# RWKV-7 recurrence in chunks: small matrix products interleaved over the four quadrants of the array, and the inverse's lanes loaded by two plain transfers

## The chip, the cores and the metric

The kernel runs on one core of one Trainium2 chip. The metric is the device time of one execution in microseconds (us), the median over several executions. The profile comes from one more execution, recorded by the hardware profiler; its engines are called PE (TensorE matmul; PEld is its weight load), DVE (VectorE), ACT (ScalarE), POOL (GpSimd) and SP (SyncE, which here only issues transfers).

## The reference, cut to what matters

A trunk of two layers on a 1024 x 1024 fp32 input (1024 tokens). The even layer has a gated MLP over chunks and a dilated attention; the odd layer is RWKV-7 time mixing with 16 heads of 64 channels. The change touches the odd layer's recurrence only:

```python
def rwkv7_scan(r, w, k, v, kk, a):            # (S, B, H, N), state (B, H, N_v, N_k)
    def step(state, inp):
        r_t, w_t, k_t, v_t, kk_t, a_t = inp
        sa = jnp.einsum('bhvk,bhk->bhv', state, -kk_t)
        state = (state * w_t[:, :, None, :]
                 + sa[..., None] * (kk_t * a_t)[:, :, None, :]
                 + v_t[..., None] * k_t[:, :, None, :])
        y_t = jnp.einsum('bhvk,bhk->bhv', state, r_t)
        return state, y_t
    _, ys = lax.scan(step, state0, (r, w, k, v, kk, a))
    return ys
```

After it come a group norm of y, a bonus term, a SiLU gate, an output projection, a residual add and a final norm.

## The kernel before, in words

The program runs in stages: the even layer to about 508 us, the odd layer's projections to about 1003 us, the recurrence to about 1390 us, then the output projection and the end. The recurrence (class `Rwkv`) doesn't go token by token. It takes the 1024 tokens in 16 chunks of 64, and turns the dependences within a chunk into a triangular 64 x 64 inverse per head. Heads are laid out as 8 pairs `q`, and in a pair head `e` (0 or 1) has partitions 64e to 64e+63. So each product of one head is 64 x 64 and uses one quadrant of the 128 x 128 array: rows are chosen by the partitions of the operands, columns by the partitions of the output. A block of such products is 16 instructions (8 pairs, 2 heads). Blocks whose head `e` goes from rows e to columns e use the two diagonal quadrants; blocks from rows e to columns 1-e, the other two.

For one chunk `c` the blocks are, with the lines of the kernel before:

- `al` (`alphas`, L1051, evacuated to M at L1052): products of A and BK for the inverse, diagonal. `ak` (`keys`, L1040, to AK at L1041): products of BK and A, off the diagonal. Both go through the PSUM tag "pt" with two buffers.
- `sc` (`scores`, L1029, to MY at L1030): 8 products of 128 x 64 for half of the pairs.
- `sM` (`store_M`, L1059): four transfers from ACT's queue put the 32 x 32 blocks of M to DRAM (MA). `lM` (`load_M`, L1098, on SP's queue) reads them back as lanes, one per partition, into Nt; a lane's 1024 numbers are contiguous, and partitions 64 to 127 hold the same as 0 to 63.
- `ia`, `ie`, `ib`, `ic`: VectorE inverts the lanes (DN at L1120, tm and R to L1163, result xm); `ic` stores xm to XT (L1170, SP), `lX` loads it as X (L1178, four transfers on SP). `mx`, `ma`, `mb` (L1184, L1196, L1209) merge the 32 x 32 blocks to the 64 x 64 inverse.
- `V` (`Wkeys`, L1223, off the diagonal) and `W` (L1230, diagonal) sum into one PSUM tile, evacuated to Ws (L1232). `U` (L1241, diagonal) applies X to Ws and is evacuated to UV (L1244). `st` (`state`, L1265, then an add on VectorE, L1267) makes the next state S; `keep` decays it on GpSimd.
- `Y` (`Yout`): L1275 from MY and UV, then L1280 from the state, then the evacuation (L1281). `Yd` stores Y (L1285, ACT's queue).

One step of the loop takes two chunks, and prepares the chunks of two steps later: its M blocks are made while the inverse of the step between is under way. The order in which every engine gets its instructions is the order of the program, written out by hand in three strings of tokens (SCAN_START, SCAN_STEP for six steps, SCAN_END); a token is a function's short name with a number. The gate projection of the odd layer is cut into pieces (`g`, L943, six or nine 128 x 512 matmuls at a time), which stand between the tokens. One inverse is in flight at a time (Nt has one buffer, X one). The six steps' strings before:

```python
SCAN_STEP = (
    "U0 V1 al0 ib2 st0 al1 sM0 uv0 Y0 keep1 ib1 W1 sc0 ib1 U1 V2 ak0 uv1 ld6 st1 sc1 ib1 ic0 dec0 Y1 lM0 W2 keep2 ip0 "
    "lX0 ak1 gx1 sc2 Yd0 T0 msk0 g2 ia0 sc3 g2 mx0 ma0 ie0 g2 dec1 T1 mb0 msk1 g3 ib3 ld7 gl2")
```

Of the kernel before, what the change touches and what calls it, by code (L numbers as in the profile page):

```python
# [11 lines left out]
AF = mybir.ActivationFunctionType  # L12
# [12 lines left out]
NC = 16  # L25
CH = 64
# [201 lines left out]
def even_layer(g, a):  # L228
# [749 lines left out]
class Rwkv:  # L978
# [39 lines left out]
    def scores(self, c, qq):  # L1018

        g, nc, t = self.g, self.g.nc, self.T[c]  # L1020
        A, BK = t["A"], t["BK"]
        if qq == 0:
            t["MY"] = self.ring("MY", c, NY, [P, NHD, CH])
        pm = self.pm[:, :, qq]
        for i in range(4):
            q = 4 * qq + i
            for e in range(2):
                r = slice(64 * e, 64 * e + 64)
                nc.tensor.matmul(pm[:, e, i], BK[r, q].rearrange("p j t -> p (j t)"), A[r, q, 1], start=True, stop=True)  # L1029
        nc.scalar.activation(t["MY"].rearrange("p (e q) t -> p e q t", e=2)[:, :, 4 * qq:4 * qq + 4], pm, AF.Copy)  # L1030

    def keys(self, c):

        g, nc, t = self.g, self.g.nc, self.T[c]
        t["AK"] = AK = self.ring("AK", c // 2, 3, [P, 2, KT, CH])[:, c % 2]
        pk = g.bC([P, KT, CH], "pt")
        for q in range(KT):
            for e in range(2):
                r, o = slice(64 * e, 64 * e + 64), slice(64 - 64 * e, 128 - 64 * e)
                nc.tensor.matmul(pk[o, q], t["BK"][r, q, 1 - e], t["A"][r, q, 0], start=True, stop=True)  # L1040
        nc.scalar.activation(AK, pk, AF.Copy)  # L1041

    def alphas(self, c):

        g, nc, t = self.g, self.g.nc, self.T[c]
        M = self.ring("M", c // 2, 2, [P, 2, KT, CH])
        pa = g.bC([P, KT, CH], "pt")
        for q in range(KT):
            for e in range(2):
                r = slice(64 * e, 64 * e + 64)  # L1050
                nc.tensor.matmul(pa[r, q], t["A"][r, q, 0], t["BK"][r, q, e], start=True, stop=True)  # L1051
        nc.scalar.activation(M[:, c % 2], pa, AF.Copy)  # L1052
# [39 lines left out]
    def load_M(self, b2):  # L1092

        g, nc, pool = self.g, self.g.nc, self.pool
        Nf = pool.tile([P, 1056], F32, name="Nt", bufs=1)
        Nt = Nf[:, 0:1024].rearrange("p (t s) -> p t s", s=32)
        m = g.MA_d[b2]
        nc.sync.dma_start(Nf[:, 0:1024], bass.AP(tensor=m.tensor, offset=m.offset, ap=[[0, 2], [1024, 64], [1, 1024]]))  # L1098
# [116 lines left out]

    def Wkeys(self, c):

        g, nc, t = self.g, self.g.nc, self.T[c]
        self.pw = g.bA([P, KT, CH], "ch")
        for q in range(KT):  # L1220
            for e in range(2):
                o, r = slice(64 * e, 64 * e + 64), slice(64 - 64 * e, 128 - 64 * e)
                nc.tensor.matmul(self.pw[o, q], t["AK"][r, q], t["UV"][r, e, q], start=q == 0, stop=False)  # L1223

    def W(self, c):
        g, nc, t = self.g, self.g.nc, self.T[c]
        for q in range(KT):
            for e in range(2):
                o = slice(64 * e, 64 * e + 64)
                nc.tensor.matmul(self.pw[o, q], t["A"][o, q, 0], t["S"][o, q],  # L1230
                                 start=False, stop=q == KT - 1)
        nc.scalar.activation(self.Ws, self.pw, AF.Copy)  # L1232

    def U(self, c):
        g, nc, t = self.g, self.g.nc, self.T[c]
        X = self.ring("X", c // 2, 1, None)
        pu = g.bA([P, KT, CH], "ch")
        for q in range(KT):
            for e in range(2):
                o = slice(64 * e, 64 * e + 64)  # L1240
                nc.tensor.matmul(pu[o, q], X[o, c % 2, q], self.Ws[o, q], start=True, stop=True)  # L1241
        for e in range(2):
            o = slice(64 * e, 64 * e + 64)
            nc.scalar.activation(t["UV"][o, e], pu[o], AF.Copy)  # L1244
# [24 lines left out]
    def Yout(self, c):  # L1269

        g, nc, t = self.g, self.g.nc, self.T[c]
        py = g.bD([P, KT, CH], "py")
        for q in range(KT):
            for e in range(2):
                nc.tensor.matmul(py[64 * e:64 * e + 64, q], t["MY"][:, 8 * e + q], t["UV"][:, e, q],  # L1275
                                 start=q == 0, stop=False)
        for q in range(KT):
            for e in range(2):
                r = slice(64 * e, 64 * e + 64)
                nc.tensor.matmul(py[r, q], t["A"][r, q, 1], t["S"][r, q], start=False, stop=q == KT - 1)  # L1280
        nc.scalar.activation(self.Y[:, c % 2], py, AF.Copy)  # L1281

    def store_Y(self, b):
        for e in range(2):
            self.g.nc.scalar.dma_start(self.g.Y_d[b].rearrange("(c t) h d -> t c h d", c=2)[:, :, 8 * e:8 * e + 8],  # L1285
                                     self.Y[64 * e:64 * e + 64])

    def start(self, gate):
        g, nc = self.g, self.g.nc

        def zs(i):
            nc.gpsimd.memset(self.new_S(0), 0.0)

        self.pm = g.bB([P, 2, 2, 4, CH], "pm")
        ops = dict(L=gate.load, wx=gate.split, xl=gate.load_x, ld=self.load,
                   g=lambda i: [next(gate.rest, None) for _ in range(i)],
                   sc=lambda i: self.scores(i // 2, i % 2), al=self.alphas, sM=self.store_M, lM=self.load_M,
                   ip=self.inverse_p, ia=self.inverse_a, ie=self.inverse_d, ib=lambda i: [next(self.rows, None) for _ in range(i)],
                   ic=self.inverse_c, lX=self.load_X, mx=self.merge_x, ma=self.merge_a, mb=self.merge_b,
                   dec=self.decayed, T=self.transposed, msk=self.masks,  # L1300
                   ak=self.keys, uv=self.load_uv, V=self.Wkeys, W=self.W, keep=self.keep, zs=zs)
        for name, i in order(SCAN_START):
            ops[name](i)

    def ops(self, b, gate):
        c = 2 * b
        return dict(
            U=lambda i: self.U(c + i), st=lambda i: self.state(c + i), keep=lambda i: self.keep(c + i),
            W=lambda i: self.W(c + i), V=lambda i: self.Wkeys(c + i), sc=lambda i: self.scores(c + 4 + i // 2, i % 2),
            al=lambda i: self.alphas(c + 4 + i), sM=lambda i: self.store_M(b + 2 + i),  # L1310
            lM=lambda i: self.load_M(b + 2 + i), ip=lambda i: self.inverse_p(b + 2 + i),
            ia=lambda i: self.inverse_a(b + 2 + i),
# [2 lines left out]
            mx=lambda i: self.merge_x(b + 1 + i), ma=lambda i: self.merge_a(b + 1 + i),  # L1315
            mb=lambda i: self.merge_b(b + 1 + i), dec=lambda i: self.decayed(c + 4 + i),
            T=lambda i: self.transposed(c + 4 + i), Y=lambda i: self.Yout(c + i),
            msk=lambda i: self.masks(c + 4 + i), ak=lambda i: self.keys(c + 4 + i),
            uv=lambda i: self.load_uv(c + 2 + i), ld=lambda i: c + i < NC and self.load(c + i),
            g=lambda i: [next(gate.rest, None) for _ in range(i)],  # L1320
            gl=lambda i: b + KT + i < 2 * KT and gate.load(b + KT + i),
# [226 lines left out]
```

## Time and profile before

| | before |
|---|---|
| median of three runs | 1547.66 us (1547.51 to 1555.07) |
| the profiled execution | 1541.35 us |
| its span | 1539.6 us |
| mean granted clock of TensorE | 0.94 |
| busy share of the span | PE 88%, DVE 57%, ACT 41%, POOL 35% |

The recurrence is a quarter of the span. The profile gives a page, and for any stretch: a timeline by engine (start, duration, line, out<-in, and in brackets the idle time ahead with what ended it), the chain of work that ended last, a table of waits, and windows with the busy time of each engine, the clock that TensorE was granted, and the share of the 16 DMA engines that was busy. A matmul row counts records; neighbouring records of one line are put together as "x32".

### The profile page before, as it was taken

The page shows a single profiled execution, that of the slowest core. Times are in us where ns is not written, and L with a number is a line of the kernel's source. Part 1 is how long each engine was busy: PE and PEld are TensorE (multiplying, and loading weights), DVE is VectorE, ACT ScalarE, POOL GpSimd, SP SyncE. Part 2 cuts the span into 40 slices and gives each one's busy share as a digit, 9 for nine tenths or more (in the row PEclk, how much of TensorE's full clock was granted, in tenths as well). Part 3 has the DMA queues.
Part 4 walks back from the last instruction along what each step waited for, and adds up shares of the span by engine and source line. Part 5 has one row for each costly group of instructions (what it writes and reads, how often), then busy time and mean ns, then how long its engine had stood idle before and what let it go on. Part 6 is the DMA issues. An engine that isn't in the chain of part 4 may idle for free.

```text
span 1539.6 us, 29856 instructions
## 1 busy us (share of the span) xinstructions
PE 1349.7 (88%) x12261; PEld 1154.1 (75%) x12261; DVE 885.2 (57%) x1489; ACT 631.7 (41%) x1188; POOL 545.9 (35%) x353
## 2 busy tenths in 40 slices
PE   5899999799979999999978799988977777687887
PEld 5887879688878899888645478967866666677886
DVE  8742446834574357615988974315554544477884
ACT  4423436533543235626454542323433333254322
POOL 8650001120216212213433531227323333357851
PEclk9999999999999999999989899989988888889899
DMA  5385444521523443241865474265744445476412
GB/s 212 100 268 152 124 155 119 138 69 53 154 82 131 138 130 98 66 140 42 232 185 124 109 206 114 64 198 135 237 118 131 111 125 139 120 222 217 139 40 96
DMA packets 253032, 209.09 MB, mean 136 GB/s; under 512 B 79408, under 2 KB 215184, under 8 KB 252896
## 3 DMA queue, kind: packets, MB, share of 16 engines
q1 hardware_dynamic: 230096, 191.98, 42.2%
q10 hardware_dynamic: 22800, 15.21, 3.6%
q8 instruction: 96, 1.57, 0.4%
q14 instruction: 40, 0.33, 0.1%
HBM read 135.71 MB, written 71.43 MB: 135 GB/s over the span
## 4 chain that ended last, share of the span: by engine, by line
PE 57%; DVE 15%; DMA 10%; issue 5%; ACT 5%; POOL 3%; SPq 3%; ACTq 1%; DVEq 0%; POOLq 0%
PE pj L153 34%; PE pj L943 3%; DMA X<-XT 3%; SPq L1178 2%; PE pj L1460 1%; PE pt L572 1%; PE pj L711 1%; PE pm L1029 1%; DMA BK<-BK_d 1%; DMA Nt<-MA 1%; PE pt L1051 1%; PE sp L559 1%; PE ch L1241 1%; PE sp L562 1%; PE op L580 1%
## 5 line engine op out<-in xcount | busy, mean ns | idle before, releaser
L106 POOL TENSOR_TENSOR wl<-wraw,wh 128x1024 fp32r<-128x1024 f32 x38 | 95.5, 2514 | 176.0 <-ACT wh L105 159.3
L153 PE MATMUL pj<-hh,wh 128*128 128x512 f32 x320 | 127.3, 398 | 0.0
L153 PE MATMUL pj<-hh,wl 128*128 128x512 f32 x320 | 126.7, 396 | 0.0
L153 PE MATMUL pj<-hl,wh 128*128 128x512 f32 x320 | 126.6, 396 | 0.0
L106 DVE TENSOR_TENSOR wl<-wraw,wh 128x1024 fp32r<-128x1024 f32 x46 | 69.8, 1523 | 87.4 <-ACT wh L105 43.8
L105 ACT ACTIVATE wh<-wraw 128x1024 fp32r<-128x1024 f32 x84 | 88.0, 1055 | 60.6 <-DMA wraw<-in_w_in_even_dram 22.2
L153 PE MATMUL pj<-xl,wh 128*128 128x512 f32 x256 | 103.2, 404 | 2.6 <-DVE xl L740 2.6
L153 PE MATMUL pj<-xh,wh 128*128 128x512 f32 x256 | 103.1, 405 | 2.5 <-ACT ks L789 2.4
L153 PE MATMUL pj<-xh,wl 128*128 128x512 f32 x256 | 102.8, 402 | 0.0
L1460 PE MATMUL pj<-wh,yh 128*128 128x256 f32 x256 | 76.9, 300 | 5.4 <-DVE x L1464 3.2
L566 DVE CUSTOM_DVE_ANT_0 sc<-sp,tb 128x128 f32<-128x128 f32 (+3 forms) x64 | 48.2, 753 | 57.7 <-PE sp L562 48.9
L1460 PE MATMUL pj<-wh,yl 128*128 128x256 f32 x256 | 75.9, 296 | 5.6 <-POOL yl L106 5.6
L153 PE MATMUL pj<-wh,hh 128*128 128x256 f32 x256 | 74.8, 295 | 2.9 <-ACT hh L265 2.6
L153 PE MATMUL pj<-wh,hl 128*128 128x256 f32 x256 | 75.0, 294 | 1.2 <-DVE hl L266 1.2
L1460 PE MATMUL pj<-wl,yh 128*128 128x256 f32 x256 | 75.5, 295 | 0.0
L737 DVE SCALAR_TENSOR_TENSOR xm<-hT,pr,xm 128x512 f32<-128x512 f32 x56 | 50.0, 934 | 44.0 <-ACT xm L736 43.6
L153 PE MATMUL pj<-wl,hh 128*128 128x256 f32 x256 | 74.4, 291 | 0.0
L153 PE MATMUL pj<-wh,yl 128*128 128x256 f32 x256 | 72.5, 283 | 1.9 <-POOL yl L624 1.9
L153 PE MATMUL pj<-wh,xh 128*128 128x256 f32 x256 | 72.9, 285 | 0.1
L153 PE MATMUL pj<-wl,xh 128*128 128x256 f32 x256 | 72.9, 285 | 0.0
L153 PE MATMUL pj<-wh,xl 128*128 128x256 f32 x256 | 72.8, 284 | 0.0
L153 PE MATMUL pj<-wh,yh 128*128 128x256 f32 x256 | 72.1, 282 | 0.5 <-ACT yh L623 0.5
(320 smaller groups left out, 4034.3 us busy)
## 6 DMA issues: line engine op xcount, KB each, us to landing
wraw<-in_w_in_even_dram SPq DMA_DIRECT2D x28, 512.0 KB
tb<-tb SPq DMA_DIRECT2D x16, 512.0 KB
A_d<-AR SPq DMA_DIRECT2D x16, 512.0 KB
wraw<-in_rw_wg_dram SPq DMA_DIRECT2D x16, 512.0 KB
A<-A_d SPq DMA_DIRECT2D x16, 512.0 KB
BK<-BK_d SPq DMA_DIRECT2D x16, 512.0 KB
xt<-in_x_dram SPq DMA_DIRECT2D x8, 512.0 KB
dv<-vt SPq DMA_DIRECT2D x16, 256.0 KB
```

The lines of the kernel that those rows point to most:

```text
L105: nc.scalar.activation(hi, raw, AF.Copy)
L106: sub.tensor_tensor(lo, raw, hi.bitcast(F32), OP.subtract)
L153: nc.tensor.matmul(ps, a(k), b(k), start=(n == 0), stop=(n == 3 * KT - 1))
L559: nc.tensor.matmul(sp[:, c0:c1], qs[:, b * P:(b + 1) * P], kh[:, c0:c1], start=True, stop=False)
L562: nc.tensor.matmul(sp[:, c0:c1], qs[:, b * P:(b + 1) * P], kl[:, c0:c1], start=False, stop=True)
L566: nc.vector.tensor_tensor_reduce(sc[:, :n], sp[:, :n], tb[:, off:off + n], 1.0, BIG, OP.add, OP.min, mn)
L572: nc.tensor.transpose(pt[:, j - j0, :], sc[:, j * P:(j + 1) * P], g.ident)
L580: nc.tensor.matmul(op[:, s0:QW], vt[:, j, :], pth[j // 4][:, j % 4, s0:QW], start=(j == 0), stop=False)
L737: nc.vector.scalar_tensor_tensor(t, hT[kk, f][:, j, 0:512], g.pr[:, i, k:k + 1], t, op0=OP.mult, op1=OP.add)
L943: nc.tensor.matmul(ps, u[:, k], v[:, k % 2], start=(k == 0 and i == 0), stop=(k == KT - 1 and i == 2))
L1178: self.g.nc.sync.dma_start(X[32 * k:32 * k + 32, :, :, 32 * b:32 * b + 32].rearrange("p c q t -> p (c q) t"), xd[k].rearrange("c q a e t - ...
L1460: nc.tensor.matmul(ps[:, i, :], u[:, k], v[:, k % 4], start=(k == 0 and j == 0), stop=(k == KT - 1 and j == 2))
```

## The change

It does three things. The load of the lanes is written as two transfers of 64 partitions x 1024 numbers instead of one with a leading dimension of 2 and stride 0. Blocks on the diagonal quadrants and blocks on the other two are issued alternately, pair by pair: `al` with `ak` of the same chunk (both now evacuated there, so the token `ak` goes away), `U` of a chunk with `V` of the next, and `W` of a chunk with the state half of `Y` of the chunk before. For the last, the halves of the PSUM tile of Y and of its store are swapped. `sc` is written as 16 products of 64 x 64 over all quadrants instead of 8 of 128 x 64.

```diff
 SCAN_STEP = (
-    "U0 V1 al0 ib2 st0 al1 sM0 uv0 Y0 keep1 ib1 W1 sc0 ib1 U1 V2 ak0 uv1 ld6 st1 sc1 ib1 ic0 dec0 Y1 lM0 W2 keep2 ip0 "
-    "lX0 ak1 gx1 sc2 Yd0 T0 msk0 g2 ia0 sc3 g2 mx0 ma0 ie0 g2 dec1 T1 mb0 msk1 g3 ib3 ld7 gl2")
+    "U0 al0 ib2 st0 al1 sM0 uv0 Y0 keep1 ib1 W1 sc0 ib1 U1 uv1 ld6 st1 sc1 ib1 ic0 dec0 Y1 lM0 W2 keep2 ip0 lX0 "
+    "gx1 sc2 Yd0 T0 msk0 g2 ia0 sc3 g2 mx0 ma0 ie0 g2 dec1 T1 mb0 msk1 g3 ib3 ld7 gl2")
...
     def scores(self, c, qq):
...
-            for e in range(2):
-                r = slice(64 * e, 64 * e + 64)
-                nc.tensor.matmul(pm[:, e, i], BK[r, q].rearrange("p j t -> p (j t)"), A[r, q, 1], start=True, stop=True)
+            for j in range(2):
+                for e in range(2):
+                    r, o = slice(64 * e, 64 * e + 64), slice(64 * (e ^ j), 64 * (e ^ j) + 64)
+                    nc.tensor.matmul(pm[o, e, i], BK[r, q, e ^ j], A[r, q, 1], start=True, stop=True)
...
     def alphas(self, c):
-        pa = g.bC([P, KT, CH], "pt")
+        t["AK"] = AK = self.ring("AK", c // 2, 3, [P, 2, KT, CH])[:, c % 2]
+        pa, pk = g.bC([P, KT, CH], "pt"), g.bC([P, KT, CH], "pt")
         for q in range(KT):
             for e in range(2):
                 r = slice(64 * e, 64 * e + 64)
                 nc.tensor.matmul(pa[r, q], t["A"][r, q, 0], t["BK"][r, q, e], start=True, stop=True)
+            for e in range(2):
+                r, o = slice(64 * e, 64 * e + 64), slice(64 - 64 * e, 128 - 64 * e)
+                nc.tensor.matmul(pk[o, q], t["BK"][r, q, 1 - e], t["A"][r, q, 0], start=True, stop=True)
         nc.scalar.activation(M[:, c % 2], pa, AF.Copy)
+        nc.scalar.activation(AK, pk, AF.Copy)
...
     def load_M(self, b2):
-        nc.sync.dma_start(Nf[:, 0:1024], bass.AP(tensor=m.tensor, offset=m.offset, ap=[[0, 2], [1024, 64], [1, 1024]]))
+        for par in range(2):
+            nc.sync.dma_start(Nf[64 * par:64 * par + 64, 0:1024], m.rearrange("k c q t s -> (k c q) (t s)"))
...
     def Wkeys(self, c):
         for q in range(KT):
...
+            yield
     def W(self, c):
+        rest = self.Ystate(c - 1) if c else iter(())
         for q in range(KT):
...
+            next(rest, None)
         nc.scalar.activation(self.Ws, self.pw, AF.Copy)
+        next(rest, None)
     def U(self, c):
+        rest = self.Wkeys(c + 1) if c < NC - 1 else iter(())
         for q in range(KT):
...
+            next(rest, None)
...
     def Yout(self, c):
...
+    def Ystate(self, c):
+        py, Y = self.py, self.Y
+        for q in range(KT):
+            for e in range(2):
+                r, o = slice(64 * e, 64 * e + 64), slice(64 - 64 * e, 128 - 64 * e)
+                nc.tensor.matmul(py[o, q], t["A"][r, q, 1], t["S"][r, q], start=False, stop=q == KT - 1)
+            if q < KT - 1:
+                yield
+        yield
+        nc.scalar.activation(Y[:, c % 2], py, AF.Copy)
```

On TensorE, the beginning of a step before, from the first U to the second (ch, pt, py and pm are PSUM tiles; MATMUL rows give output <- operands):

```order
L1241 MATMUL ch<-Ws,X 64x64 x16
L1223 MATMUL ch<-UV,AK 64x64 x16
L1051 MATMUL pt<-BK,A 64x64 x16
L1265 MATMUL ch<-UV,BKT 64x64 x16
L1051 MATMUL pt<-BK,A 64x64 x16
L1275 MATMUL py<-UV,MY 64x64 x16
L1280 MATMUL py<-S,A 64x64 x16
L1230 MATMUL ch<-S,A 64x64 x16
L1029 MATMUL pm<-A,BK 128x64 x8
L1241 MATMUL ch<-Ws,X 64x64 x16
```

In the changed kernel every block of 16 that has a partner is cut into twos, which alternate with its partner's; this is where the second U with V ends, and the following W with the state half of Y begins:

```order
L1246 MATMUL ch<-Ws,X 64x64 x2
L1221 MATMUL ch<-UV,AK 64x64 x2
L1271 MATMUL ch<-UV,BKT 64x64 x16
L1030 MATMUL pm<-A,BK 64x64 x16
L1281 MATMUL py<-UV,MY 64x64 x16
L1231 MATMUL ch<-S,A 64x64 x2
L1290 MATMUL py<-S,A 64x64 x2
```

V is no longer a block of its own between U and the state's product (L1265 before, L1271 now), nor is `ak`, which stood there in the second half of the step. On SP's queue, at the end of an inverse in the middle of a step (store of XT, load of the next lanes, load of X, loads of the next chunks):

```order
 L1003 DMA BK<-BK_d 128x1024
-L1170 DMA XT_138<-xm 1024x1x32 x2
-L1098 DMA Nt<-MA_131 128x1x1024
-L1178 DMA X<-XT_138 32x16x32 x4
+L1167 DMA XT_138<-xm 1024x1x32 x2
+L1095 DMA Nt<-MA_131 64x1024 x2
+L1175 DMA X<-XT_138 32x16x32 x4
 L1001 DMA A<-A_d 128x1024
```

The places on the queue stay; only the load of the lanes has become two. On ACT, between the first and the second U's evacuation of a step, before:

```order
L1244 ACTIVATE UV<-ch 64x512 x2
L1052 ACTIVATE M<-pt 128x512 x2
L1059 DMA MA_132<-M 32x16x32 x4
L1281 ACTIVATE Y<-py 128x512
L1232 ACTIVATE Ws<-ch 128x512
L1030 ACTIVATE MY<-pm 128x2x256
```

and now:

```order
L1250 ACTIVATE UV<-ch 64x512 x2
L1047 ACTIVATE M<-pt 128x512
L1048 ACTIVATE AK<-pt 128x512
L1047 ACTIVATE M<-pt 128x512
L1048 ACTIVATE AK<-pt 128x512
L1055 DMA MA_132<-M 32x16x32 x4
L1234 ACTIVATE Ws<-ch 128x512
L1294 ACTIVATE Y<-py 128x512
L1031 ACTIVATE MY<-pm 128x2x256
```

Two evacuations of AK have come ahead of the stores of M, and the evacuation of Y has moved behind that of Ws.

More of the change, by code (lines that the diff above doesn't have):

```diff
@@ L1026, in scores @@
             q = 4 * qq + i
-            for e in range(2):
-                r = slice(64 * e, 64 * e + 64)
-                nc.tensor.matmul(pm[:, e, i], BK[r, q].rearrange("p j t -> p (j t)"), A[r, q, 1], start=True, stop=True)
+            for j in range(2):
+                for e in range(2):
+                    r, o = slice(64 * e, 64 * e + 64), slice(64 * (e ^ j), 64 * (e ^ j) + 64)
+                    nc.tensor.matmul(pm[o, e, i], BK[r, q, e ^ j], A[r, q, 1], start=True, stop=True)
         nc.scalar.activation(t["MY"].rearrange("p (e q) t -> p e q t", e=2)[:, :, 4 * qq:4 * qq + 4], pm, AF.Copy)
[L1032 to L1041, printed above, removed]
     def alphas(self, c):
@@ L1218, in Wkeys @@
         g, nc, t = self.g, self.g.nc, self.T[c]
-        self.pw = g.bA([P, KT, CH], "ch")
+        self.pw = pw = g.bA([P, KT, CH], "ch")
         for q in range(KT):
@@ L1222, in Wkeys @@
                 o, r = slice(64 * e, 64 * e + 64), slice(64 - 64 * e, 128 - 64 * e)
-                nc.tensor.matmul(self.pw[o, q], t["AK"][r, q], t["UV"][r, e, q], start=q == 0, stop=False)
+                nc.tensor.matmul(pw[o, q], t["AK"][r, q], t["UV"][r, e, q], start=q == 0, stop=False)
+            yield
     def W(self, c):
         g, nc, t = self.g, self.g.nc, self.T[c]
+        rest = self.Ystate(c - 1) if c else iter(())
         for q in range(KT):
@@ L1271, in Yout @@
         g, nc, t = self.g, self.g.nc, self.T[c]
-        py = g.bD([P, KT, CH], "py")
+        self.py = g.bD([P, KT, CH], "py")
         for q in range(KT):
             for e in range(2):
-                nc.tensor.matmul(py[64 * e:64 * e + 64, q], t["MY"][:, 8 * e + q], t["UV"][:, e, q],
+                nc.tensor.matmul(self.py[64 - 64 * e:128 - 64 * e, q], t["MY"][:, 8 * e + q], t["UV"][:, e, q],
                                  start=q == 0, stop=False)
+    def Ystate(self, c):
+        g, nc, t = self.g, self.g.nc, self.T[c]
+        py, Y = self.py, self.Y
         for q in range(KT):
             for e in range(2):
-                r = slice(64 * e, 64 * e + 64)
-                nc.tensor.matmul(py[r, q], t["A"][r, q, 1], t["S"][r, q], start=False, stop=q == KT - 1)
-        nc.scalar.activation(self.Y[:, c % 2], py, AF.Copy)
+                r, o = slice(64 * e, 64 * e + 64), slice(64 - 64 * e, 128 - 64 * e)
[4 more added lines that the diff above has]
+        nc.scalar.activation(Y[:, c % 2], py, AF.Copy)
     def store_Y(self, b):
@@ L1285, in store_Y @@
             self.g.nc.scalar.dma_start(self.g.Y_d[b].rearrange("(c t) h d -> t c h d", c=2)[:, :, 8 * e:8 * e + 8],
-                                     self.Y[64 * e:64 * e + 64])
+                                     self.Y[64 - 64 * e:128 - 64 * e])
     def start(self, gate):
@@ L1300, in start @@
                    dec=self.decayed, T=self.transposed, msk=self.masks,
-                   ak=self.keys, uv=self.load_uv, V=self.Wkeys, W=self.W, keep=self.keep, zs=zs)
+                   uv=self.load_uv, V=lambda i: list(self.Wkeys(i)), W=self.W, keep=self.keep, zs=zs)
         for name, i in order(SCAN_START):
@@ L1308, in ops @@
             U=lambda i: self.U(c + i), st=lambda i: self.state(c + i), keep=lambda i: self.keep(c + i),
-            W=lambda i: self.W(c + i), V=lambda i: self.Wkeys(c + i), sc=lambda i: self.scores(c + 4 + i // 2, i % 2),
+            W=lambda i: self.W(c + i), sc=lambda i: self.scores(c + 4 + i // 2, i % 2),
             al=lambda i: self.alphas(c + 4 + i), sM=lambda i: self.store_M(b + 2 + i),
@@ L1317, in ops @@
             T=lambda i: self.transposed(c + 4 + i), Y=lambda i: self.Yout(c + i),
-            msk=lambda i: self.masks(c + 4 + i), ak=lambda i: self.keys(c + 4 + i),
+            msk=lambda i: self.masks(c + 4 + i), R=lambda i: list(self.Ystate(c + i)),
             uv=lambda i: self.load_uv(c + 2 + i), ld=lambda i: c + i < NC and self.load(c + i),
```

18 rows, old and new, of tables (SCAN_END, SCAN_START) are left out of this document.

## The prediction

> **What bounds the kernel now.** I read the page first (TensorE busy 88% of the span), then the granted clock, the chain of waits, the table of waits and the queue timeline of the recurrence only, because the change touches nothing else. The chain of waits gives the recurrence's period. These are the first and the last of five consecutive starts of the merge's first product (L1196), with the pieces that follow one of them; columns are start, duration, what.
>
> ```profile
> 1124.69 1.91 PE pt L1196 x62
> ...
> 1134.23 0.90 PE ch L1241 x26
> ...
> 1136.83 1.08 PE ch L1265 x32
> ...
> 1146.02 0.93 PE pt L1040 x32
> ...
> 1148.03 1.04 PE pm L1029 x16
> ...
> 1153.96 1.02 PE pt L1076 x8
> 1154.99 1.38 PE pj L943 x6
> ...
> 1167.94 1.91 PE pt L1196 x62
> 1169.86 2.86 PE pj L943 x6
> 1172.71 1.58 PE pt L1076 x8
> ...
> 1177.74 0.90 PE ch L1241 x26
> ...
> 1296.44 1.91 PE pt L1196 x62
> ```
>
> A step (two chunks) takes (1296.44 − 1124.69)/4 = 42.94 us. I cut it in three: **b**, from the first U (1134.23) to the issue of the inverse's store XT; **c**, from that issue to the merge; **a**, from the merge to the next U (1177.74 − 1167.94 = 9.8). The queue of SP, with start and duration:
>
> ```profile
> 1150.72 1.27 SPq L1170 DMA_DIRECT2D XT<-xm  x2
> 1152.09 0.56 SPq L1098 DMA_DIRECT2D Nt<-MA  x1
> 1154.36 8.96 SPq L1178 DMA_DIRECT2D X<-XT  x4
> ```
>
> So b = 1150.72 − 1134.23 = 16.5 and c = 1167.94 − 1150.72 = 17.2. In c the four small X loads alone hold SP for 8.96 us, and the lanes' load Nt stands ahead of them. The table of waits of 1003 to 1390 us shows who waits (total, times, longest), and the windows show busy time of PE, PEld, DVE, ACT, POOL, then granted clock, DMA share, GB/s:
>
> ```profile
> DVE DN L1120 <- DMA Nt<-MA: 100.5, 7, 35.7
> PE pt L1196 <- DMA X<-XT: 47.0, 10, 9.0
> ```
>
> ```profile
> 1134.20:1150.70 16.50, 15.52 (x469) 14.77 (x470) 9.55 (x12) 6.33 (x11) 3.27 (x2) 1.00 0.39 116
> ...
> 1159.00:1167.40 8.40, 0.00 (x0) 0.02 (x1) 0.43 (x2) 0.00 (x0) 5.73 (x6) 0.79 0.23 64
> 1167.40:1174.00 6.60, 6.34 (x78) 5.47 (x78) 6.00 (x22) 1.57 (x3) 0.00 (x0) 0.50 0.92 275
> ...
> 1159.00:1163.00 4.00, 0.00 (x0) 0.00 (x0) 0.00 (x0) 0.00 (x0) 3.92 (x4) 1.00 0.13 53
> 1168.00:1170.00 2.00, 2.00 (x63) 1.94 (x64) 1.83 (x8) 0.11 (x1) 0.00 (x0) 0.50 0.98 360
> ```
>
> Three things are to be seen. TensorE stands still for 8.4 us per step, waiting for X. It then works at clock 0.50: the merge takes 1.91 and six gate matmuls 2.86, against 1.38 at full clock. And while everything waits, the DMA engines are almost idle: share 0.13 is 2 of 16 engines, 53 GB/s, which is Nt with its leading dimension of 2 (the A and BK loads just after, 128 rows each, get 0.98 and 360). X is queued on engines that are full of Nt. The last pass of the recurrence has no Nt load, so it shows c without one:
>
> ```profile
> 1364.96 1.26 SPq L1170 DMA_DIRECT2D XT<-xm  x2
> 1370.08 1.94 SPq L1178 DMA_DIRECT2D X<-XT  x4
> ...
> 1375.00 1.20 PE L1196 MATMUL pt<-X,M 32*32 32x32 f32 x64
> ```
>
> The X issue takes 1.94 instead of 8.96, and the merge starts, without a wait, 10.04 us after XT's issue.
>
> **The change, part by part.**
>
> *Nt by two loads of 64 rows.* Each has 64 rows outermost, so I expect it on all engines: 512 KB at the 360 GB/s above is 1.5 us (estimate) instead of the 14.8 from issue (1152.09) to the row that waits for it:
>
> ```profile
> 1166.87 0.42 DVE L1120 TENSOR_TENSOR DN<-Nt,rn 128x256 f32<-128x256 f32 x1 [11.09 <-DMA Nt<-MA]
> ```
>
> SP issues one transfer more, 0.5 us by the row of Nt, beside XT's own flight: X still starts 3.64 after XT (1154.36 − 1150.72). Then 1.94 for its issue and at most 1375.00 − (1370.08 + 1.94) = 2.98 for its landing give 8.6; the last pass gives 10.04; unchanged would be 17.2. I take c = 9.5, near the measured pass, and keep 8.6 to 11. TensorE has less to do before the merge too, so 3 to 4 us of idle remain.
>
> *Clock in a.* At full clock, a is shorter by 1.91 − 1.20 (merge, against the last pass), 2.86 − 1.38 (six gate matmuls) and 1.58 − 1.02 (L1076, rows of the first fence): 9.8 − 2.75 = 7.1. Whether the clock falls depends on the idle that is left. The start of the recurrence has such a gap:
>
> ```profile
> 1077.26 0.21 PE L1196 MATMUL pt<-X,M 32*32 32x32 f32 x2 [3.83 <-DMA X<-XT]
> 1077.79 1.42 PE L1196 MATMUL pt<-X,M 32*32 32x32 f32 x61 [0.31 <-DMA X<-XT]
> ```
>
> After 3.83 us the merge took 1.42, between 1.20 and 1.91. I take a = 7.8 (7.1 to 9.8).
>
> *Pairs: U with the next chunk's V, al with ak, W with the state half of Y.* A block of 32 records (16 products) holds TensorE for 1.08 us (the L1265 row of the chain). Where U ends and V begins, the timeline of TensorE reads:
>
> ```profile
> 1135.03 0.22 PE L1223 MATMUL ch<-UV,AK 64*64 64x64 f32 x1
> 1135.03 0.22 PE L1241 MATMUL ch<-Ws,X 64*64 64x64 f32 x1
> ...
> 1135.09 0.22 PE L1241 MATMUL ch<-Ws,X 64*64 64x64 f32 x1
> 1135.09 0.27 PE L1223 MATMUL ch<-UV,AK 64*64 64x64 f32 x2
> ```
>
> Both start within the same hundredths of a microsecond, U on the diagonal quadrants and V on the other two. So I take 1.08 us for 64 paired records; unpaired they cost 2.16. Six pairs per step save 6 × 1.08 = 6.5 us of TensorE work. Most of it only lengthens the idle ahead of the merge, where TensorE waits for X anyhow. What lies on the path is in b, where ScalarE decides:
>
> ```profile
> 1135.36 1.20 ACT L1244 ACTIVATE UV<-ch 64x512 f32<-64x512 f32 x2 [1.18 <-PE ch L1241]
> 1136.88 0.60 ACT L1052 ACTIVATE M<-pt 128x512 f32<-128x512 f32 x1 [0.33 <-PE pt L1051]
> 1139.04 0.60 ACT L1052 ACTIVATE M<-pt 128x512 f32<-128x512 f32 x1 [1.56 <-PE pt L1051]
> 1139.67 3.26 ACTq L1059 DMA_DIRECT2D MA<-M  x4
> 1142.97 0.60 ACT L1281 ACTIVATE Y<-py 128x512 f32<-128x512 f32 x1 [3.33 <-DMA MA<-M]
> 1143.46 0.59 ACT L1232 ACTIVATE Ws<-ch 128x512 f32<-128x512 f32 x1
> ```
>
> The second U needs Ws. Ahead of it now come two more evacuations (AK, 0.6 each); the second M is ready one block (0.5 to 1.08) earlier, unless its PSUM buffer waits for AK's first evacuation; and Y moves behind Ws (0.5 less). That is 9.9 ± 0.5 from U to U, as before (the four MA issues, 3.26, stay). From the second U on, V (1.08) and AK (0.93, the L1040 row) no longer stand ahead of the state product, but that one waits for UV, so 0.4 of it comes through to the state's addition, and behind it the inverse's last row and XT. I take b = 16.1, with 15.5 and 16.6 as ends. VectorE is late next: in the windows above it is busy 6.00 of 6.60 us right after the merge and 9.55 of 16.5 in b. Its next transpose waits for X in the middle of the inverse, so it runs beside TensorE with little to spare, and I don't put the step lower than that sum.
>
> *Scores as 16 products of 64x64 instead of 8 of 128x64.* A group holds TensorE 1.04 us (the L1029 row); 16 products of the other blocks hold it 1.08. So each group costs nothing, and if its products ran at half that pace, 1 us more, of which one group of the four stands between the second U and XT: the bad end is +1 per step.
>
> *The start and the first step.* The first inverse waits for the first Nt, and X for the inverse:
>
> ```profile
> 1020.25 14.59 DMA Nt<-MA
> ```
>
> Nt lands some 9 us earlier; TensorE, which works until 3.83 before the merge (above), has four key blocks less (4 × 1.08 = 4.3), so the merge comes 3.8 + 4.3 = 8 earlier (3.8 to 10). The first step (1124.69 − 1077.79 = 46.9 us) also waits for loads that stay: 7 saved, of 4 to 9.5.
>
> **The sum.** Steady step: 9.5 + 7.8 + 16.1 = 33.4, saving 9.5 in each of five steps: 47. The last step already has no Nt: 0. With 8 and 7 that is 62. The profiled execution took 1541.35 (span 1539.6), 6.3 below the median of 1547.66; 1541.35 − 62 = 1479.4, and 1485.7 against the median: I say 1486. Its own range, with steps of 31.5 to 35.5, is 1472 to 1500.
>
> **Rivals.** (1) *Also warm.* If little enough idle remains, the clock stays at 1.00: 8.6 + 7.1 + 15.5 = 31.2, saving 5 × 11.7 + 15 = 74, so 1474. For it the short gap; against it VectorE's order. 0.12.
> (2) *Pairs gain nothing.* If paired products run one after another, a pair of blocks takes 2.16: the second U comes 2.2 later, its tail 2 later: 37.5, saving 5 × 5.4 + 4 + 5 = 36, so 1512. The rows at 1135.03 speak against it. 0.13. The Trainium skill, "TensorE: Matmul & The Clock Gate", Part 3, says that a weight load overlaps running matmuls only when its row group differs; V and U share row groups, so by it the time would be this 1512. The trace disagrees where it shows the case: the L1223 rows at 1135.03 start among those of L1241.
> (3) *X's own small packets are the slow part,* and c falls only to 14: 37.9, saving 5 × 5 + 8 + 4 = 37, so 1511. Against it the last pass (10.04, with gate matmuls running). 0.09.
> (4) *The load doesn't spread:* 1538 to 1548, since b and c stay. 0.04.
> (5) *Slower: each turn from one pair of quadrants to the other drains the array.* A pair of blocks has 16 turns, and five pairs lie on the path (U with V twice, al with ak twice, W once). It eats the gain of 9.5 when each costs 1.9 more than 2.16, that is at 0.25 us per turn; at 0.27, the duration of the L1223 row at 1135.09, a step is 1.3 longer, seven steps 9 us: 1557. The rows at 1135.03 show turns without it. 0.04.
>
> **How the numbers follow.** The forecast has 0.58, and these the rest. The range holds it, (1), and both of (2) and (3); its low end is steps of 30 with the upper ends of start and first step (5 × 12.9 + 19.5 = 84): 1464 to 1514. A measurement here can tell about 0.5%, 7.7 us, from no change. Faster holds the forecast and (1) to (3): 0.92; half of (4) and some of (5) are same: 0.04; slower 0.04.
>
> **What would show it.** Right: the wait of L1120 for Nt ends 4 to 6 us after Nt's issue; the four X issues take about 2; idle before the merge 3 to 4; merges 33.4 apart; 64 paired records in about 1.1 us; the second U 9.9 after the first. Wrong: an X issue that still takes over 5 us, paired blocks of 2.1, a second U later than 11, or VectorE as the releaser of the state and merge with steps of 36 or more.

## The result and the profile after

| | before | changed |
|---|---|---|
| median | 1550.18 us (1547.51 to 1555.07, 4 runs) | 1487.55 us (1486.46 to 1489.41, 4 runs) |
| profiled execution | 1541.35 us, span 1539.6 | 1486.46 us, span 1484.4 |
| mean granted clock | 0.94 | 0.943 |
| busy per span | PE 1349.7, DVE 885.2 us | PE 1305.9, DVE 913.4 us |

The ratio is 0.9594 (95% interval 0.9564 to 0.9624): the kernel became faster by 4.1%. A second set of five runs gave 1487.63 and 0.9621 (0.9597 to 0.9646).

The chain of waits of the changed kernel has the merge's first product (now L1193) at these starts (start, duration, what):

```profile
1110.87 1.91 PE pt L1193 x62
...
1147.41 1.91 PE pt L1193 x62
...
1182.93 1.19 PE pt L1193 x62
...
1217.46 1.33 PE pt L1193 x62
...
1252.85 1.91 PE pt L1193 x34
```

Four steps between the first and the last: 35.5 us each, against 42.94. SP's queue in one of these steps (XT, lanes, X), and two rows of the table of waits of 1003 to 1390 us (total, times, longest):

```profile
1137.68 1.43 SPq L1167 DMA_DIRECT2D XT<-xm  x2
1139.21 1.28 SPq L1095 DMA_DIRECT2D Nt<-MA  x2
1141.33 3.52 SPq L1175 DMA_DIRECT2D X<-XT  x4
```

```profile
DVE DN L1117 <- DMA Nt<-MA: 44.3, 6, 29.8
PE pt L1193 <- DMA X<-XT: 16.3, 9, 3.1
```

The four X issues take 1.9 to 3.6 us in the seven passes that have a load of lanes, instead of 6.9 to 9.0, VectorE's wait for the lanes has fallen from 100.5 to 44.3 us in all (29.8 of them the first one) and TensorE's for X from 47.0 to 16.3. The timeline of TensorE inside a pair, U (L1246) with V (L1221):

```profile
1157.29 0.23 PE L1246 MATMUL ch<-Ws,X 64*64 64x64 f32 x2
1157.30 0.23 PE L1221 MATMUL ch<-UV,AK 64*64 64x64 f32 x2
1157.35 0.23 PE L1246 MATMUL ch<-Ws,X 64*64 64x64 f32 x2
1157.36 0.23 PE L1221 MATMUL ch<-UV,AK 64*64 64x64 f32 x2
```

Two records of each start every 0.06 us, on all four quadrants. So 64 records take the time that 32 took.

The table gives means over the same five steps of each profile (second to seventh merge), put together from starts like those above; a is merge to first U, b first U to XT's issue, c XT's issue to the merge. The times of a row are from one profiled execution, its ratio from all runs. Where X arrives in two parts, the merge is counted from the larger one, as in the chain.

| kernel | step | a | b | c | ratio to before (95%) |
|---|---|---|---|---|---|
| before | 42.95 | 9.77 | 16.05 | 17.13 | 1 |
| predicted | 33.4 | 7.8 | 16.1 | 9.5 | |
| changed | 35.16 | 9.26 | 16.33 | 9.58 | 0.9594 (0.9564 to 0.9624) |
| two loads alone | 35.18 | 9.41 | 15.84 | 9.93 | 0.9629 (0.9595 to 0.9664) |
| pairs and scores alone | 42.90 | 9.59 | 15.75 | 17.57 | 0.9996 (0.9975 to 1.0018) |
| two transfers by columns | 43.86 | 9.93 | 16.20 | 17.73 | 1.0005 (0.9983 to 1.0026) |
| gate pieces early | 33.85 | 5.91 | 18.09 | 9.85 | 0.9569 (0.9539 to 0.9599) |
| changed, old scores | 36.24 | 9.07 | 16.96 | 10.21 | 0.9647 (0.9620 to 0.9674) |
| gate early, masks moved | 33.80 | 5.56 | 17.63 | 10.61 | 0.9571 (0.9550 to 0.9593) |
| and stores of M later | 34.26 | 5.45 | 18.42 | 10.39 | 0.9616 (0.9596 to 0.9636) |
| changed, masks moved | 35.62 | 9.42 | 15.96 | 10.24 | 0.9634 (0.9607 to 0.9661) |
| changed, again | 35.50 | 9.40 | 16.42 | 9.68 | 0.9621 (0.9597 to 0.9646) |
| gate pieces early, again | 33.79 | 5.70 | 18.23 | 9.87 | 0.9599 (0.9571 to 0.9627) |
| two loads, al with ak | 35.30 | 9.05 | 16.20 | 10.06 | 0.9648 (0.9625 to 0.9671) |

### The profile page after: what moved, and what is told of

The parts are those of the page before. It is cut to its first block, busy times and chain, and to the rows that moved or that the text cites. A ratio compares the mean times of both kernels' runs of the same rounds, so it can differ in the third digit from the quotient of the medians.

```text
span 1484.4 us, 30909 instructions
## 1 busy us (share of the span) xinstructions
PE 1305.9 (88%) x12773; PEld 1110.6 (75%) x12773; DVE 913.4 (62%) x1489; ACT 628.8 (42%) x1188; POOL 544.7 (37%) x353
## 4 chain that ended last, share of the span: by engine, by line
PE 51%; DVE 17%; DMA 12%; ACT 7%; issue 6%; POOL 4%; SPq 2%; ACTq 1%; DVEq 0%; POOLq 0%
PE pj L153 33%; PE pj L943 3%; PE pt L572 2%; PE pj L1473 2%; PE pj L711 2%; DMA X<-XT 1%; DMA XT<-xm 1%; DMA w<-in_rw_a_dram 1%; DMA BK<-BK_d 1%; PE ch L1271 1%; PE op L580 1%; ACT wh L105 1%; PE sp L559 1%; PE sp L562 1%; ACT UV L1250 1%
## 5 line engine op out<-in xcount | busy, mean ns | idle before, releaser
L1473 PE MATMUL pj<-wl,yh 128*128 128x256 f32 x256 | 73.8, 288 | 0.0
L153 PE MATMUL pj<-wl,yh 128*128 128x256 f32 x256 | 72.9, 285 | 0.0
```

Source lines behind the costliest of these rows:

```text
L153: nc.tensor.matmul(ps, a(k), b(k), start=(n == 0), stop=(n == 3 * KT - 1))
L1473: nc.tensor.matmul(ps[:, i, :], u[:, k], v[:, k % 4], start=(k == 0 and j == 0), stop=(k == KT - 1 and j == 2))
```

## The experiments

### The load or the pairs

Two kernels take the change apart. The first is the kernel before with only this edit:

```diff
-        nc.sync.dma_start(Nf[:, 0:1024], bass.AP(tensor=m.tensor, offset=m.offset, ap=[[0, 2], [1024, 64], [1, 1024]]))
+        for par in range(2):
+            nc.sync.dma_start(Nf[64 * par:64 * par + 64, 0:1024], m.rearrange("k c q t s -> (k c q) (t s)"))
```

> The kernel before, with only the load of the lanes written as two transfers of 64 partitions; blocks, tokens and scores as before. Theory (the load carries nearly all of the gain): the four X issues take 2 to 3.5 us, the row that waits for Nt starts 5 to 6 us after Nt's issue instead of 14.8, the path from XT's issue to the merge falls from 17.2 to about 10; TensorE, which has some 6 us more to do per step than in the changed kernel, stands still for 0 to 2 us before the merge; steps of 35.5 to 37, ratio to before 0.960 to 0.970. Rival (the pairs carry a good part, because TensorE or the wait for Ws is on the path): steps of 38 to 39, ratio 0.975 to 0.985.

Measured: 1493.11 us, ratio 0.9629 (0.9595 to 0.9664). SP's queue and the waits of this kernel:

```profile
1177.86 1.93 SPq L1171 DMA_DIRECT2D XT<-xm  x2
1179.90 1.25 SPq L1099 DMA_DIRECT2D Nt<-MA  x2
1182.02 2.21 SPq L1179 DMA_DIRECT2D X<-XT  x4
```

```profile
DVE DN L1121 <- DMA Nt<-MA: 41.4, 7, 29.7
...
PE pt L1197 <- DMA X<-XT: 6.6, 8, 1.7
```

The second kernel is the changed one with that edit undone:

```diff
-        for par in range(2):
-            nc.sync.dma_start(Nf[64 * par:64 * par + 64, 0:1024], m.rearrange("k c q t s -> (k c q) (t s)"))
+        nc.sync.dma_start(Nf[:, 0:1024], bass.AP(tensor=m.tensor, offset=m.offset, ap=[[0, 2], [1024, 64], [1, 1024]]))
```

> The changed kernel with the old load of the lanes (one transfer, leading dimension of 2, stride 0). Theory (the load carries nearly all): the path from XT's issue to the merge stays near 17, TensorE stands still for 11 to 13 us before the merge because its work has become shorter, steps of 42 to 43.5, ratio 0.990 to 1.000. Rival (the pairs carry a good part): steps of 39 to 41, ratio 0.97 to 0.985.

Measured: 1546.67 us, ratio 0.9996 (0.9975 to 1.0018). Its table of waits has TensorE standing longer for X than in any other kernel:

```profile
PE pt L1192 <- DMA X<-XT: 68.6, 8, 14.9
```

One step of each kernel as a window (busy time of PE, PEld, DVE, ACT, POOL; clock; DMA share; GB/s): the kernel before, the pairs alone, the two loads alone, the changed kernel, a fence for each.

```profile
1212.20:1254.30 42.10, 33.89 (x747) 29.94 (x747) 20.55 (x38) 15.49 (x26) 14.90 (x15) 0.86 0.46 126
```

```profile
1171.00:1212.70 41.70, 28.51 (x813) 24.39 (x813) 21.05 (x38) 14.86 (x26) 15.49 (x15) 0.83 0.49 128
```

```profile
1188.40:1221.70 33.30, 31.05 (x747) 27.66 (x747) 24.41 (x43) 15.29 (x26) 14.33 (x16) 1.00 0.60 157
```

```profile
1182.90:1217.50 34.60, 25.18 (x813) 21.47 (x815) 26.16 (x41) 14.85 (x26) 16.40 (x17) 1.00 0.61 164
```

Both times came as the first theory had it. (Two sizes were a little off: the steps with the two loads alone are just under the 35.5 to 37 expected, and TensorE's idle time ahead of the merge, 8.8 to 11.8 us with the pairs alone, is at the lower end or under the 11 to 13 expected.) The pairs take 5 to 6 us of TensorE's work out of a step (33.89 to 28.51), and the step stays at 42.90: what is saved ahead of the merge is waited for at X. With the two loads alone the step is 35.18, that of the changed kernel 35.16. The pairs and scores are worth something only outside the steps, as far as these two executions show it: to the first merge (1077.2 with the loads alone, 1069.8 in the changed kernel) and behind the last (164.6 us to the end of the span against 159.2). Less 1.4 and 2.9 us that its first and last steps are longer, this makes up the 8.5 us between the two spans. Between the medians it is 1493.11 to 1487.55, and the intervals of the two ratios overlap.

### What of the old load was slow

The kernel before, with two transfers of all 128 partitions, each of half the columns:

```diff
-        nc.sync.dma_start(Nf[:, 0:1024], bass.AP(tensor=m.tensor, offset=m.offset, ap=[[0, 2], [1024, 64], [1, 1024]]))
+        for h in range(0, 1024, 512):
+            nc.sync.dma_start(Nf[:, h:h + 512],
+                              bass.AP(tensor=m.tensor, offset=m.offset + h, ap=[[0, 2], [1024, 64], [1, 512]]))
```

> The kernel before, with the load of the lanes as two transfers of 128 partitions x 512 numbers, each still with the leading dimension of 2 and stride 0. Theory (the leading dimension of 2 keeps the transfer on 2 engines): the DMA share stays near 0.13 while Nt is under way, the row that waits for Nt starts 13 to 16 us after the issue, X issues take 7 to 9 us, ratio 0.995 to 1.005. Rival (what counts is that there are two transfers): 5 to 7 us after the issue, X issues of 2 to 3.5, ratio 0.96 to 0.97.

Measured: 1548.09 us, ratio 1.0005 (0.9983 to 1.0026). SP's queue:

```profile
1153.06 1.18 SPq L1099 DMA_DIRECT2D Nt<-MA  x2
1155.17 9.85 SPq L1180 DMA_DIRECT2D X<-XT  x4
```

In the steps the row that waits for Nt starts 13.6 to 15.0 us after the issue, and X's issue takes 7.4 to 9.9. Two transfers with the leading dimension of 2 are as slow as one, so it isn't the number of transfers. Together with the prediction's rows (share 0.13 for 53 GB/s, which is two engines' worth; the trace has two packets in flight at a time there) this says that the load ran on two engines because of its leading dimension, and that the X loads were issued slowly because they came behind it. That dimension has both a size of 2 and a stride of 0; no run separates the two.

### Why merge to U stayed long

The changed kernel with five gate pieces moved from behind the merge's products to ahead of them:

```diff
-    "gx1 sc2 Yd0 T0 msk0 g2 ia0 sc3 g2 mx0 ma0 ie0 g2 dec1 T1 mb0 msk1 g3 ib3 ld7 gl2")
+    "gx1 sc2 Yd0 T0 msk0 g2 ia0 sc3 g7 mx0 ma0 ie0 dec1 T1 mb0 msk1 ib3 ld7 gl2")
```

> The changed kernel with five gate pieces (15 matmuls of 0.235 us at full clock, 3.5 us) moved from behind the merge's two products to the stretch ahead of them, where TensorE stands still for 2.9 to 3.7 us. Theory (the stretch from merge to U stayed at 9.3 instead of 7.8 because the clock falls in that wait and the cold merge and gate pieces follow): idle before the merge under 1 us, the merge takes 1.2 to 1.4, merge to U 6 to 7.5, steps of 33 to 34, time 1472 to 1480, ratio to before 0.949 to 0.955. Rival (VectorE: its transpose for the merge comes 3 to 4.5 us after the merge's start and its inverse fills the step, so that what is won before U is waited for at the state): steps stay at 35 to 35.5, time 1485 to 1489, ratio 0.958 to 0.961.

Measured: 1482.62 us, ratio 0.9569 (0.9539 to 0.9599). The stretch right behind the merge as windows (the clock is the third number from the end), of the changed kernel and of this one:

```profile
1147.40:1153.40 6.00, 5.99 (x75) 5.24 (x76) 5.68 (x13) 1.52 (x3) 4.25 (x5) 0.50 0.84 265
```

```profile
1144.40:1150.00 5.60, 3.96 (x136) 3.22 (x136) 5.32 (x11) 3.55 (x6) 4.46 (x5) 1.00 1.01 328
```

Merge to U fell by 3.4 us (a is 5.91, just under the 6 to 7.5 expected), but the step by only 1.3: U to U grew from 9.0 to 11.4. The fall of a alone doesn't show the clock, since the five gate pieces that left this stretch are 3.5 us at full clock; the clock of 1.00 in the window does. The steps (33.85) are those of the first theory, the time lies between what the two theories gave.

The masks tell the clock from VectorE. In the changed kernel VectorE's first rows of an inverse look like this, with GpSimd's rows of the same time behind them:

```profile
1144.66 0.91 DVE L1127 TENSOR_TENSOR tm<-DN 128x4 f32<-128x4 f32 x1
1145.61 0.16 DVE L1129 TENSOR_REDUCE DN<-tm 128x4 f32<-128x4 f32 x1
...
1146.44 1.79 DVE L1127 TENSOR_TENSOR tm<-DN 128x36 f32<-128x36 f32 x1
1148.26 0.19 DVE L1129 TENSOR_REDUCE DN<-tm 128x12 f32<-128x36 f32 x1
```

```profile
1144.17 1.40 POOL L1078 TENSOR_SCALAR_AFFINE_SELECT MY<-MY 64x1024 f32<-64x1024 f32 x1
...
1146.26 1.91 POOL L1062 TENSOR_TENSOR BK<-BK,EC 128x1024 f32<-128x1024 f32 x1
```

Each two-input row ends when GpSimd's instruction does (1145.57 and 1148.23, against 1145.57 and 1148.17), however small it is; the reductions between them, with one input, keep their 0.16 to 0.19. The changed kernel with the masks elsewhere (a step's first ones ahead of the next inverse's blanks, the second ones behind the next step's decay):

```diff
-    "U0 ... keep1 ib1 W1 ... W2 keep2 ip0 lX0 gx1 sc2 Yd0 T0 msk0 g2 ia0 ... T1 mb0 msk1 g3 ib3 ld7 gl2")
+    "U0 ... keep1 mp0 ib1 W1 ... W2 keep2 msk0 ip0 lX0 gx1 sc2 Yd0 T0 g2 ia0 ... T1 mb0 g3 ib3 ld7 gl2")
...
+            mp=lambda i: c and self.masks(c + 3),
```

> The changed kernel with GpSimd's masks moved as in the sixth, and the gate pieces where the changed kernel has them. It tells apart what kept the stretch from the merge to U at 9.3 us. Theory (the half clock after the wait for X, on the merge and the gate pieces behind it): VectorE's transposes come about 2 us earlier, and nothing else moves: merge to U 9 to 10, steps of 34.5 to 36, ratio to before 0.957 to 0.962. Rival (VectorE's late transposes hold the second product of the merge): merge to U 7 to 8, steps of 33 to 34, ratio 0.949 to 0.955.

Measured: 1489.65 us, ratio 0.9634 (0.9607 to 0.9661). The transposes come 1.2 us after the merge's start instead of 2.6 (means of five), and a is 9.42: VectorE didn't hold it. In the five steps of the changed kernel a is 9.51, 9.72, 7.91, 9.32 and 9.83; the 7.91 belongs to the merge at 1182.93, the only one with full clock behind it:

```profile
1182.90:1188.90 6.00, 5.13 (x142) 4.47 (x143) 5.72 (x11) 3.10 (x6) 5.62 (x6) 1.00 0.99 322
1217.50:1223.50 6.00, 5.75 (x114) 4.76 (x116) 5.69 (x12) 2.86 (x5) 4.61 (x5) 0.72 0.98 275
1252.80:1258.80 6.00, 5.95 (x75) 5.21 (x76) 5.66 (x13) 1.47 (x3) 4.69 (x5) 0.50 0.98 316
```

So it is the clock: the shorter wait for X still costs it in four steps of five. Counting the five steps each of the changed kernel, of its repeat (below) and of this one, a is 9.3 to 9.9 us at the twelve merges before which TensorE waited 3.2 to 4.6 us in all, and 7.9 to 8.7 at the three with 0 to 1.6.

### Where the early gate pieces' gain went

The same masks on top of the early gate pieces:

> The fourth kernel (gate pieces ahead of the merge) with GpSimd's masks moved: those of a step's first chunk ahead of the blanks of the next inverse, those of its second chunk behind the first decay of the next step. Theory (VectorE's two-input rows at the beginning of an inverse stand still while a GpSimd instruction runs, 0.9 to 1.8 us instead of 0.2, since the lanes now arrive when GpSimd masks): these rows fall to 0.2 to 0.4, the transposes for the merge come 1 to 3 us earlier, the first addition to the state is no longer 3.8 us behind its product; the first U to the second falls from 11.4 to 10 or less; steps of 31 to 32.5, ratio to before 0.943 to 0.951. Rival (the four stores of M and Ws on ScalarE hold the second U anyway): steps of 33 to 34, ratio 0.954 to 0.958.

Measured: 1482.28 us, ratio 0.9571 (0.9550 to 0.9593), no better. The rows themselves did as expected. VectorE's groups by form between 1110 and 1300 us (busy, mean ns), of the kernel before, the changed one, and this one:

```profile
L1130 DVE TENSOR_TENSOR tm<-DN 128x36 f32<-128x36 f32 x5 | 1.0, 197 | 0.2
```

```profile
L1127 DVE TENSOR_TENSOR tm<-DN 128x36 f32<-128x36 f32 x6 | 6.8, 1137 | 0.2
```

```profile
L1127 DVE TENSOR_TENSOR tm<-DN 128x36 f32<-128x36 f32 x5 | 1.0, 196 | 0.2
```

The first addition to the state comes at 11.9 us after the merge instead of 14, yet U to U is still 10.8 (11.4 without), and steps and ratio are the rival's (33 to 34, 0.954 to 0.958). The rival's reason was that the second U waits for Ws, and Ws for the four stores of M on ScalarE's queue. So those were moved behind Ws:

```diff
-    "U0 al0 ib2 st0 al1 sM0 uv0 Y0 keep1 mp0 ib1 W1 sc0 ...
+    "U0 al0 ib2 st0 al1 uv0 Y0 keep1 mp0 ib1 W1 sM0 sc0 ...
```

> The kernel with moved masks, and the four stores of M on ScalarE's queue (2.6 to 3.3 us) moved from ahead of the evacuation of Ws to behind it. Theory (those stores stand on the path from the first U to the second): U to U falls by another 1.5 to 3, steps of 29 to 31, ratio to before 0.932 to 0.943. Rival (VectorE or TensorE sets the second U by then, or M's later arrival delays the next lanes): within 0.5 us per step of the kernel with moved masks.

Measured: 1488.21 us, ratio 0.9616 (0.9596 to 0.9636), slower than without. U to U fell by 0.4 only and b grew by 0.8, so the stores did not hold the second U, and the theory missed here too. The steps are 0.46 us longer, within the rival's 0.5. What binds b once a is short was not found.

### Scores, al with ak, and a repeat

The changed kernel with the scores as before:

```diff
-            for j in range(2):
-                for e in range(2):
-                    r, o = slice(64 * e, 64 * e + 64), slice(64 * (e ^ j), 64 * (e ^ j) + 64)
-                    nc.tensor.matmul(pm[o, e, i], BK[r, q, e ^ j], A[r, q, 1], start=True, stop=True)
+            for e in range(2):
+                r = slice(64 * e, 64 * e + 64)
+                nc.tensor.matmul(pm[:, e, i], BK[r, q].rearrange("p j t -> p (j t)"), A[r, q, 1], start=True, stop=True)
```

> The changed kernel with the scores as before (8 products of 128x64 per group instead of 16 of 64x64). In the changed kernel TensorE pauses nine times between 1050 and 1345 us inside its small products without a wait on anything (10.1 us in all, four of them at the scores, 4.7 us); the kernel before has none. Each pause ends 2 to 3 us after a 16 KB packet of the instruction queue began. Theory (blocks of four quadrants use up code faster than it is fetched): with 8 products instead of 16 per group the pauses at the scores go, 2 to 5 pauses of 2 to 6 us in all stay, at the pairs; a group takes 1.04 instead of 0.65 us; together no change of time that can be told, ratio to before 0.956 to 0.963. Rival (the pauses have nothing to do with the number of instructions, and the 64x64 form is the faster one): pauses as before, steps 1 to 2 us longer, ratio 0.963 to 0.970.

Measured: 1494.66 us, ratio 0.9647 (0.9620 to 0.9674). TensorE's pauses (last section) came as the theory on code had it, none at the scores: five at the pairs and at Y (3.5 us), and one of 1.56 us inside the merge's second product. The time did not: the steps are 1.1 us longer and the first merge is at 1077.4 instead of 1069.8, as the rival had it. So the 64x64 form is probably the better one, pauses included; the ratio's interval overlaps a little with the changed kernel's first (0.9564 to 0.9624) and more with its second (0.9597 to 0.9646).

The kernel before with the two loads, and al paired with ak (`alphas` as in the changed kernel, `keys` and the tokens `ak` gone):

```diff
-    "U0 V1 al0 ... U1 V2 ak0 uv1 ... lX0 ak1 gx1 ...
+    "U0 V1 al0 ... U1 V2 uv1 ... lX0 gx1 ...
```

> The kernel before with the two loads, and al paired with ak (one evacuation of AK behind each of M), but U, V, W, Y and the scores as before. The changed kernel came 7.4 us earlier to the first merge than the one with the two loads alone, and 5.4 us were saved behind the last. Theory (TensorE bounds the start of the recurrence, where four blocks of ak are 4.3 us of its work): the first merge comes 3 to 6 us earlier than 1077.2, at 1071 to 1074, the steps stay at 35 to 36, ratio to before 0.959 to 0.963. Rival (the pairs of U with V or the scores' form won it): first merge at 1076 to 1078, ratio 0.963 to 0.966.

Measured: 1492.76 us, ratio 0.9648 (0.9625 to 0.9671), the first merge at 1074.3: 2.9 of the 7.4 us, in one execution. The kernels that share the changed kernel's start have this merge anywhere from 1067.9 to 1073.1, so 2.9 is within what executions differ by. The time is not distinguishable from that of the loads alone.

The changed kernel and the one with early gate pieces, once more on one chip:

> The changed kernel once more, on the same chip as the next one. 1486 to 1490 us, ratio to before 0.957 to 0.962.

> The kernel with the gate pieces ahead of the merge once more. Theory (it is really 1.3 us per step shorter): 5 to 9 us under the changed kernel of the same chip, 1479 to 1483. Rival (the difference seen was between chips or executions): within 3 us of it.

Measured: 1487.63 (0.9621) and 1484.33 us (0.9599, 0.9571 to 0.9627): 3.3 us apart, 4.9 in the first sets. That lies between the two theories. The steps are 1.7 and 1.3 us shorter in the two pairs of profiles (35.50 to 33.79, 35.16 to 33.85), the medians differ by 3 to 5 us, and the intervals overlap. Early gate pieces, with or without the masks moved, are the best version found, by a margin that the ratios don't settle.

## Why the prediction was right

The time (1487.55 against 1486) and the mechanism were right; the terms agreed less well than the total.

- *c, right.* 9.58 against 9.5, from the pass without a lane load. Nt to the row that waits for it takes 4.9 to 6.3 us, predicted 4 to 6.
- *b, right in size.* 16.33 against 16.1, and U to U 9.0 against 9.9. The means of before are 16.05 and 9.4, though: the prediction read one step (16.5 and 9.9), and the 0.4 us that the pairs were to take off b did not show.
- *Pairs hidden, right.* 64 records in the time of 32, no effect in the steps.
- *a, mis-sized.* 9.26 against 7.8. The step that failed is "I take a = 7.8", which rested on the one merge of 1.42 us behind a wait of 3.83. The waits before the five merges were 4.5, 3.7, 0.8, 4.1 and 3.2 us; behind the four long ones the stretch ran at half clock for 3.4 us or more. That is 1.5 us in each of five steps. The merge's own duration was too short a piece to look at: in the kernel before the clock fell at 1078.5, in the middle of that merge, and stayed at half until 1081.9, and the next U came 9.4 us after it (1077.79 to 1087.18). The two loads alone have the same instructions there, without the wait and at full clock, and U comes 7.9 us after the merge. The window of before behind that merge:

```profile
1080.00:1087.00 7.00, 7.00 (x113) 5.53 (x112) 4.77 (x16) 3.33 (x5) 1.94 (x3) 0.87 0.87 315
```

- *VectorE next, not borne out.* I had it wait for X and run with little to spare. Its busy time per step did rise from 20.6 to 23 to 26 us, in part because its small rows now meet GpSimd's masks, which was not in the working; with early gate pieces, moving the masks took it from 24.7 to 23.5, and where the rest comes from was not followed. But it set nothing: moving the masks gained no time, neither alone nor with early gate pieces.
- *The start, right size, wrong parts.* The first merge came 8.0 us earlier, as predicted, but not by the two terms named. The load alone gave 0.6, not 3.8: it was issued 3.7 us later than before (1023.96), the row that waits for it started 8.8 us after that, and so the lanes came 2.2 us earlier and not 9. Al with ak gave 2.9 more, not 4.3; all pairs with the old scores gave nothing (1077.4). These parts don't add up, and kernels with one and the same start differ by up to 5 us, so only the whole is clear. The first step gave 5.8 of 7.
- *The last step and the end, taken as 0.* The last step became 2.9 us longer (35.6 to 38.5), and the stretch from the last merge to the end of the span 5.4 shorter (164.6 to 159.2). The shorter end came with the pairs of U with V and W with Y, or with the order of the end's string, where a Y now stands ahead of a W: it is 164.6 with the loads alone, 164.9 with al and ak paired too, and 160.7 with all pairs and the old scores. The last step is less clear: the kernels with all pairs have it at 35.0 to 39.6.

The terms sum to 62; between the two profiled executions it is 54.9, with 39 from the five steps instead of 47. Between the medians it is 62.6. The profiled execution of before lay 8.8 us under its median, that of the changed kernel 1.1 under its own, so it is luck that the forecast of 1486 is as close as it is: a sum 7 us too large met an offset of 6.3 us that the changed kernel's runs hardly have. A sum from one execution is no better than that.

Of the rivals, that pairs gain nothing was half true: they run side by side, so its mechanism is not what these rows show, and they are still worth nothing in a step. The rule of the Trainium skill, "TensorE: Matmul & The Clock Gate", Part 3, that the prediction set beside it is not what these rows show either. X's small packets were not slow by themselves. The load did spread: its row starts 4.9 to 6.3 us after the issue instead of 13.5 to 14.8. No turn between quadrants cost anything (0.06 us per four records).

## What to carry to other kernels

Here a transfer with a leading dimension of 2 was slow by itself (13.5 to 14.8 us to the row that waits, instead of 4.9 to 6.3), and the small transfers queued behind it were issued slowly too; the sign was a DMA share of 0.13 while an engine waited. Work taken off an engine that waits for a transfer afterwards is not time saved: 5 us per step of it moved nothing while the transfer was long, and nothing once it was short. After such a fix, look at what the early arrival now coincides with (here the masks), and whether the wait that is left still lowers the clock (here the twelve of 3.2 us and more, in the three traces counted above, did). To price a lower clock, measure the whole stretch behind the wait, not its first instruction.

## What the runs showed of the hardware

*VectorE behind GpSimd.* A two-input row of 0.2 us took 0.4 to 1.8 us when a GpSimd instruction ran, and ended with it (rows above; 1.79 for 0.20 is the largest). The Trainium skill, "SBUF — State Buffer", in "SBUF: two separate sides", states this: the pair of ports is locked for a whole instruction by whichever starts first, VectorE's operations with two SBUF inputs among those concerned, against a GpSimd instruction that reads SBUF. The traces agree, the reductions with one input included.

*TensorE waits for code.* TensorE pauses inside blocks of small products, most often in the paired kernels, without a wait on anything; the chain shows one as "issue":

```profile
1235.51 0.06 PE ch L1221 x2
1235.59 0.04 PE ch L1221 x2
...
1235.76 1.02 issue
1236.78 0.27 PE ch L1246
```

Between 1050 and 1345 us there are 10 such pauses over 0.25 us in the changed kernel (10.4 us), 8 with the pairs alone (6.2), 6 with the old scores (5.0), 2 with the two loads alone (2.4, of which 2.12 in one, inside the merge's second product of 32x32 tiles) and none before. So they are not peculiar to the pairs, but the pairs have more of them. Every one ends 2.2 to 2.9 us after a 16 KB packet of the instruction queue began, and only 47 such packets began in this stretch of the changed kernel. Its trace has 100 packets for 25546 matmuls and weight loads, about 255 for each. A pair of blocks uses 8 (four matmuls, four weight loads) per 0.058 us, so a packet's worth in 1.9 us (an estimate from these counts), less than the 2.2 to 2.9. The Trainium skill, "Runtime: NRT & Kernel Launch", in "Instruction fetch mechanics", says that the fetch of blocks of 256 instructions is hidden because instructions are dispatched more slowly than they arrive; in these blocks the trace differs. That the pauses are the fetch is inferred from this coincidence and from the run with fewer instructions in the scores; the fetch alone was not changed.
